# A top-2 gate that writes each row twice: rows dealt to partitions in eight contiguous blocks, stores of 8 MB, and a max/min tournament for the top two

## The chip, the cores and the metric

The kernel runs on one core of a Trainium2 chip. The metric is the device time of one execution in microseconds; before the change the median of three runs is 247.52 us (246.92 to 250.12). The profile below is one execution, whose span from the first to the last instruction is 244.7 us.

## The reference

There are 16 x 1,024 = 16,384 rows. Each has 512 numbers in `x` and 8 router logits. The two largest softmax probabilities of a row are scaled to sum to one, and the row of `x` is written out twice, once times each of the two.

```python
def reference(x, router_logits, k):          # x (16,1024,512), logits (16,1024,8), k = 2
    logits_max = np.max(router_logits, axis=-1, keepdims=True)
    probs = np.exp(router_logits - logits_max)
    probs = probs / np.sum(probs, axis=-1, keepdims=True)
    topk_indices = np.argsort(probs, axis=-1)[..., -k:]
    topk_probs = np.take_along_axis(probs, topk_indices, axis=-1)
    topk_probs = topk_probs / np.sum(topk_probs, axis=-1, keepdims=True)
    x_expanded = x[:, :, np.newaxis, :].repeat(k, axis=2)
    return (x_expanded * topk_probs[..., np.newaxis]).astype(np.float32)
```

So 33.6 MB of `x` and 0.5 MB of logits are read, and 67.1 MB are written. With two chosen, the weights are sigmoids of plus and minus the difference of the two largest logits; the smaller one comes first.

## The kernel before

Rows are dealt to the 128 partitions in one piece: partition p holds the 128 rows from 128p on. In HBM one partition's rows of `x` are 256 KB, of the output 512 KB, and that is the step from one partition to the next in each load and store.

The logits come with one load on the SP queue (line 49), 4 KB per partition. VectorE (DVE in the profile) then finds the two largest of each row in four operations over 1,024 elements per partition: the maximum (line 54), a mask of where it is (58), the logits with the maximum pushed down (62), and the maximum again (54). A subtraction gives `dlt` (71), and ScalarE (ACT) makes the two weights `WA` by sigmoids (74 and 77).

The main loop has 16 steps. Each loads 8 rows per partition of `x` into a tile `xg`, 2 MB in 128 pieces of 16 KB, on the SP queue (line 101); 16 multiplies on VectorE, one for each row and slot, write `og` (line 106); and one store from the ACT queue (line 111) sends `og`, 4 MB in 128 pieces of 32 KB. There are four buffers for `xg` and three for `og`, kept by tile pools.

The order is set by these buffers. SP issues the load of step c + 4 when the multiplies of step c are done; VectorE begins step c + 3 when the store of step c has landed; ACT issues a store when its multiplies are done. Each engine works through its own list in order, so an instruction that waits holds up all that stand behind it. Loads and stores are on two DMA queues, in the profile q1 (SP) and q10 (ACT), which share the same 16 DMA engines; 8 of a transfer's 128 partition rows fall to each of them.

Of the kernel before, what the change touches and what calls it, by code (L numbers as in the profile page):

```python
# [1 line left out]

# [4 lines left out]


@with_exitstack  # L10
def kernel(
    ctx: ExitStack,
    tc: tile.TileContext,
    x: bass.AP,
    router_logits: bass.AP,
    k: bass.AP,
    out: bass.AP,
):
    nc = tc.nc
    P = 128  # L20

    B, S, D = x.shape
    E = router_logits.shape[-1]
    K = int(k)
    N = B * S

    assert N % P == 0
    M = N // P
    assert E <= 64
    assert 2 <= K <= E  # L30

    x_v = x.rearrange("b s d -> (b s) d").rearrange("(p m) d -> p m d", p=P)
    o_v = out.rearrange("b s k d -> (b s) (k d)").rearrange(
        "(p m) d -> p m d", p=P
    )
    rl_v = router_logits.rearrange("b s e -> (b s) e").rearrange(
        "(p m) e -> p m e", p=P
    )

    wpool = ctx.enter_context(tc.tile_pool(name="wpool", bufs=1))  # L40

    L = 8
    assert M % L == 0
    NCH = M // L
    xbufs = ctx.enter_context(tc.tile_pool(name="xbufs", bufs=4))
    obufs = ctx.enter_context(tc.tile_pool(name="obufs", bufs=3))

    logits = wpool.tile([P, M, E], mybir.dt.float32)
    nc.sync.dma_start(logits, rl_v)

    V = wpool.tile([P, M, K], mybir.dt.float32)
    cur = logits
    for i in range(K):
        nc.vector.reduce_max(V[:, :, i : i + 1], cur, axis=mybir.AxisListType.X)  # L54
        if i < K - 1:
            eq = wpool.tile([P, M, E], mybir.dt.float32, tag=f"eq{i}")
            nxt = wpool.tile([P, M, E], mybir.dt.float32, tag=f"nxt{i}")
            nc.vector.tensor_tensor(  # L58
                eq, cur, V[:, :, i : i + 1].to_broadcast([P, M, E]),
                op=mybir.AluOpType.is_ge,  # L60
            )
            nc.vector.scalar_tensor_tensor(  # L62
                nxt, eq, -1.0e30, cur,
                op0=mybir.AluOpType.mult, op1=mybir.AluOpType.add,
            )
            cur = nxt

    WA = wpool.tile([P, K, M], mybir.dt.float32)
    if K == 2:
        dlt = wpool.tile([P, M], mybir.dt.float32)  # L70
        nc.vector.tensor_tensor(  # L71
            dlt, V[:, :, 0], V[:, :, 1], op=mybir.AluOpType.subtract
        )
        nc.scalar.activation(  # L74
            WA[:, 1, :], dlt, mybir.ActivationFunctionType.Sigmoid, scale=1.0
        )
        nc.scalar.activation(  # L77
            WA[:, 0, :], dlt, mybir.ActivationFunctionType.Sigmoid, scale=-1.0
        )
    else:  # L80
        Em = wpool.tile([P, M, K], mybir.dt.float32)
        nc.vector.tensor_tensor(
            Em, V, V[:, :, 0:1].to_broadcast([P, M, K]),
            op=mybir.AluOpType.subtract,
        )
        nc.scalar.activation(Em, Em, mybir.ActivationFunctionType.Exp)
        Ssum = wpool.tile([P, M], mybir.dt.float32)
        nc.vector.reduce_sum(Ssum, Em, axis=mybir.AxisListType.X)
        Rinv = wpool.tile([P, M], mybir.dt.float32)
        nc.vector.reciprocal(Rinv, Ssum)  # L90
        for slot in range(K):
            nc.vector.tensor_tensor(
                WA[:, slot, :],
                Em[:, :, K - 1 - slot],
                Rinv,
                op=mybir.AluOpType.mult,
            )

    for c in range(NCH):
        xg = xbufs.tile([P, L, D], mybir.dt.float32, tag="xg")  # L100
        nc.sync.dma_start(xg, x_v[:, c * L : (c + 1) * L, :])
        og = obufs.tile([P, L, K * D], mybir.dt.float32, tag="og")
        for l in range(L):
            m = c * L + l
            for slot in range(K):
                nc.vector.tensor_scalar_mul(  # L106
                    og[:, l, slot * D : (slot + 1) * D],
                    xg[:, l, :],
                    WA[:, slot, m : m + 1],
                )  # L110
        nc.scalar.dma_start(o_v[:, c * L : (c + 1) * L, :], og)  # L111


# [1 line left out]
_INS = ['x', 'router_logits', 'k']  # L115
_OUTS = [((16, 1024, 2, 512), 'float32')]
#: Inputs that are plain numbers.
_NUMBERS = {'k': 2}


# [26 lines left out]
```

## Time and profile before

| what | time or amount |
|---|---|
| median of three runs | 247.52 us |
| span of the profiled execution | 244.7 us |
| VectorE busy | 107.8 us, 44% of the span |
| of it the 256 multiplies of line 106 | 102.6 us, 480 ns each |
| ScalarE busy | 1.8 us |
| moved by DMA | 101.2 MB, 414 GB/s over the span |
| logits, from issue to landing | 3.4 us |
| x tile of 2 MB, from issue to landing, median | 47.0 us |
| store of 4 MB, from issue to landing, median | 36.5 us |
| first multiply starts | 9.85 us |
| first store issued | 16.31 us |

The page has the busy time of each engine, then the span in 40 equal slices, in which each digit is the busy share in tenths, then the DMA queues with their packets, bytes and the share that their packets took of the time of 16 DMA engines. A packet is the piece that a DMA engine moves at once; one semaphore write of 4 bytes per engine and transfer is counted as a packet too. A table by stretches gives for each stretch its length, the busy time of three engines with the number of instructions, the clock of TensorE (not used here), the share of time in which DMA engines were busy, and the rate in GB/s. The waits say which instruction waited for what, for how long in total, how often, and how long at most.

### The profile page before, as it was taken

The numbers are of one execution on the slowest core, as the hardware profiler recorded it, in microseconds if no ns is written. First come the engines' busy times: TensorE is split into PE (matmuls) and PEld (weight loads), VectorE is DVE, ScalarE is ACT, GpSimd is POOL, SyncE is SP. The second block draws the span as 40 slices with busy tenths as digits, with TensorE's granted clock in tenths as the row PEclk, the third lists the DMA queues.
The fourth block names the chain that finished last, engine by engine and source line by source line (L and its number), as shares of the span: only waits on it lengthen the run. The fifth ranks groups of instructions, "written<-read, shape, count | busy, mean of one in ns | idle before, by whom it ended". The sixth has DMA issues, their size and how long they took to land.

```text
span 244.7 us, 383 instructions
## 1 busy us (share of the span) xinstructions
DVE 107.8 (44%) x261; ACT 1.8 (1%) x3; POOL 0.2 (0%) x4
## 2 busy tenths in 40 slices
DVE  3999708155190641807237081551906409081000
ACT  2000000000000000000000000000000000000000
POOL 0000000000000000000000000000000000000000
DMA  7999999999999999999999999999999999999980
GB/s 279 431 431 351 469 402 435 426 429 447 426 415 439 434 434 439 412 415 463 399 423 426 429 462 421 426 437 426 466 421 394 437 453 429 429 429 429 429 375 32
DMA packets 4754, 101.21 MB, mean 414 GB/s; under 512 B 528, under 2 KB 528, under 8 KB 656
## 3 DMA queue, kind: packets, MB, share of 16 engines
q10 hardware_dynamic: 2304, 67.11, 63.8%
q1 hardware_dynamic: 2448, 34.08, 33.3%
q14 instruction: 2, 0.02, 0.0%
HBM read 34.08 MB, written 67.11 MB: 414 GB/s over the span
## 4 chain that ended last, share of the span: by engine, by line
DMA 74%; DVE 15%; issue 0%; DVEq 0%; ACT 0%; ACTq 0%
DMA out_dram<-og 54%; DMA xg<-in_x_dram 19%; DVE og L106 13%; DMA logits<-in_router_logits_dram 1%; DVE V L54 1%; DVE nxt L62 1%; DVE eq L58 1%; DVEq L142 0%; ACT WA L74 0%; DVE dlt L71 0%; DVEq L106 0%; ACTq L111 0%
## 5 line engine op out<-in xcount | busy, mean ns | idle before, releaser
L106 DVE TENSOR_SCALAR og<-xg,WA 128x512 f32<-128x512 f32 x256 | 102.6, 480 | 109.3 <-DMA out_dram<-og 108.9
L54 DVE TENSOR_REDUCE V<-logits 128x128 f32<-128x1024 f32 x1 | 1.2, 1219 | 4.2 <-DMA logits<-in_router_logits_dram 4.2
L74 ACT ACT_TABLE_LOAD x1 | 1.3, 1283 | 0.7 <-PEq L128 0.7
L62 DVE SCALAR_TENSOR_TENSOR nxt<-eq,logits 128x1024 f32<-128x1024 f32 x1 | 1.2, 1226 | 0.0
L58 DVE TENSOR_TENSOR eq<-logits,V 128x1024 f32<-128x1024 f32 x1 | 1.2, 1225 | 0.0
L54 DVE TENSOR_REDUCE V<-nxt 128x128 f32<-128x1024 f32 x1 | 1.2, 1220 | 0.0
L74 ACT ACTIVATE WA<-dlt 128x128 f32<-128x128 f32 x1 | 0.3, 309 | 7.5 <-DVE dlt L71 7.5
L71 DVE TENSOR_TENSOR dlt<-V 128x128 f32<-128x128 f32 x1 | 0.3, 292 | 0.0
L77 ACT ACTIVATE WA<-dlt 128x128 f32<-128x128 f32 x1 | 0.3, 292 | 0.0
L128 POOL MEMSET const-bfloat16-1.0<- 128x1 bf16 x1 | 0.1, 102 | 0.0
L128 POOL MEMSET const-uint8-127<- 128x1 uint8 x1 | 0.1, 102 | 0.0
L128 POOL MEMSET const-float32-0.0<- 128x1 f32 x1 | 0.1, 99 | 0.2 <-issue 0.2
L128 POOL MEMSET const-float32-1.0<- 128x1 f32 x1 | 0.1, 99 | 0.0
## 6 DMA issues: line engine op xcount, KB each, us to landing
out_dram<-og ACTq DMA_DIRECT2D x16, 4096.0 KB, 36.5
xg<-in_x_dram SPq DMA_DIRECT2D x16, 2048.0 KB, 47.0
logits<-in_router_logits_dram SPq DMA_DIRECT2D x1, 512.0 KB, 3.4
```

The lines of the kernel that those rows point to most:

```text
L54: nc.vector.reduce_max(V[:, :, i : i + 1], cur, axis=mybir.AxisListType.X)
L58: nc.vector.tensor_tensor(eq, cur, V[:, :, i : i + 1].to_broadcast([P, M, E]), op=mybir.AluOpType.is_ge,)
L62: nc.vector.scalar_tensor_tensor(nxt, eq, -1.0e30, cur, op0=mybir.AluOpType.mult, op1=mybir.AluOpType.add,)
L71: nc.vector.tensor_tensor(dlt, V[:, :, 0], V[:, :, 1], op=mybir.AluOpType.subtract)
L74: nc.scalar.activation(WA[:, 1, :], dlt, mybir.ActivationFunctionType.Sigmoid, scale=1.0)
L77: nc.scalar.activation(WA[:, 0, :], dlt, mybir.ActivationFunctionType.Sigmoid, scale=-1.0)
L106: nc.vector.tensor_scalar_mul(og[:, l, slot * D : (slot + 1) * D], xg[:, l, :], WA[:, slot, m : m + 1],)
L128: nc = _bacc.Bacc("TRN2", target_bir_lowering=False, num_devices=1)
```

## The change

The rows are dealt anew. The output is cut into eight blocks of 2,048 rows, and within a block partition p holds 16 rows in succession. One store is then one block: 8 MB that lie in HBM without a break, in 128 pieces of 64 KB. It takes 16 rows of `og` per partition, so `og` is twice as large and has two buffers instead of three; two `xg` tiles of 8 rows (as large as before, four buffers as before) fill one `og`. In HBM, the step from one partition to the next becomes 32 KB for `x` and 64 KB for the output. The logits must be dealt in the same way, and their load has 8 pieces of 512 B per partition instead of one of 4 KB.

The two largest logits are found by a tournament: halves of the eight are compared by maximum and minimum, then halves of these, so that after three rounds the first and the second stand alone. That is 2 + 4 + 4 operations on 512, 256 and 128 elements per partition. The sigmoids are as before, in the other order. The branch for more than two choices, which did not run here, is gone.

The change is meant to let stores write the output in large contiguous stretches, with fewer and larger pieces, and to find the top two with less work.

```diff
+def top2_weights(nc, pool, logits, M, E):
+    hi, lo, n = None, None, E
+    while n > 1:
+        n //= 2
+        if hi is None:
+            a, b = logits[:, :, 0:n], logits[:, :, n : 2 * n]
...
+            nc.vector.tensor_tensor(nhi, a, b, op=ALU.max)
+            nc.vector.tensor_tensor(nlo, a, b, op=ALU.min)
+        else:
+            a, b = hi[:, :, 0:n], hi[:, :, n : 2 * n]
...
+            nc.vector.tensor_tensor(tmp, lo[:, :, 0:n], lo[:, :, n : 2 * n], op=ALU.max)
+            nc.vector.tensor_tensor(nlo, a, b, op=ALU.min)
+            nc.vector.tensor_tensor(nlo, nlo, tmp, op=ALU.max)
+            nc.vector.tensor_tensor(nhi, a, b, op=ALU.max)
+        hi, lo = nhi, nlo
...
+    LS = 16
+    LX = 8
+    A = M // LS
+    x_v = x.rearrange("b s d -> (b s) d").rearrange("(a p m) d -> a p m d", a=A, p=P)
     o_v = out.rearrange("b s k d -> (b s) (k d)").rearrange(
-        "(p m) d -> p m d", p=P
+        "(a p m) d -> a p m d", a=A, p=P
     )
     rl_v = router_logits.rearrange("b s e -> (b s) e").rearrange(
-        "(p m) e -> p m e", p=P
+        "(a p m) e -> p a m e", a=A, p=P
     )
...
-    obufs = ctx.enter_context(tc.tile_pool(name="obufs", bufs=3))
+    obufs = ctx.enter_context(tc.tile_pool(name="obufs", bufs=2))
...
-    nc.sync.dma_start(logits, rl_v)
+    nc.sync.dma_start(logits.rearrange("p (a m) e -> p a m e", a=A), rl_v)
+    WA = top2_weights(nc, wpool, logits, M, E)
...
-    for c in range(NCH):
-        xg = xbufs.tile([P, L, D], mybir.dt.float32, tag="xg")
-        nc.sync.dma_start(xg, x_v[:, c * L : (c + 1) * L, :])
-        og = obufs.tile([P, L, K * D], mybir.dt.float32, tag="og")
-        for l in range(L):
-            m = c * L + l
-            for slot in range(K):
-                nc.vector.tensor_scalar_mul(
-                    og[:, l, slot * D : (slot + 1) * D],
-                    xg[:, l, :],
-                    WA[:, slot, m : m + 1],
-                )
-        nc.scalar.dma_start(o_v[:, c * L : (c + 1) * L, :], og)
+    for a in range(A):
+        og = obufs.tile([P, LS, 2 * D], F32, tag="og")
+        for h in range(LS // LX):
+            xg = xbufs.tile([P, LX, D], F32, tag="xg")
+            nc.sync.dma_start(xg, x_v[a, :, h * LX : (h + 1) * LX, :])
+            for l in range(LX):
+                r = h * LX + l
+                m = a * LS + r
+                for slot in range(2):
+                    nc.vector.tensor_scalar_mul(
+                        og[:, r, slot * D : (slot + 1) * D],
+                        xg[:, l, :],
+                        WA[:, slot, m : m + 1],
+                    )
+        nc.scalar.dma_start(o_v[a], og)
```

More of the change, by code (lines that the diff above doesn't have):

```diff
@@ L7 @@
 from concourse._compat import with_exitstack
+F32 = mybir.dt.float32
+ALU = mybir.AluOpType
+ACTF = mybir.ActivationFunctionType
+P = 128
+def top2_weights(nc, pool, logits, M, E):
[4 more added lines that the diff above has]
+            a, b = logits[:, :, 0:n], logits[:, :, n : 2 * n]
+            nhi = pool.tile([P, M, n], F32, tag=f"hi{n}")
+            nlo = pool.tile([P, M, n], F32, tag=f"lo{n}")
+            nc.vector.tensor_tensor(nhi, a, b, op=ALU.max)
+            nc.vector.tensor_tensor(nlo, a, b, op=ALU.min)
+        else:
+            a, b = hi[:, :, 0:n], hi[:, :, n : 2 * n]
+            nhi = pool.tile([P, M, n], F32, tag=f"hi{n}")
+            nlo = pool.tile([P, M, n], F32, tag=f"lo{n}")
+            tmp = pool.tile([P, M, n], F32, tag=f"tmp{n}")
+            nc.vector.tensor_tensor(tmp, lo[:, :, 0:n], lo[:, :, n : 2 * n], op=ALU.max)
[3 more added lines that the diff above has]
+        hi, lo = nhi, nlo
+    dlt = pool.tile([P, M], F32, tag="dlt")
+    nc.vector.tensor_tensor(dlt, hi[:, :, 0], lo[:, :, 0], op=ALU.subtract)
+    WA = pool.tile([P, 2, M], F32, tag="WA")
+    nc.scalar.activation(WA[:, 0, :], dlt, ACTF.Sigmoid, scale=-1.0)
+    nc.scalar.activation(WA[:, 1, :], dlt, ACTF.Sigmoid, scale=1.0)
+    return WA
 @with_exitstack
@@ L19 @@
     nc = tc.nc
-    P = 128
     B, S, D = x.shape
     E = router_logits.shape[-1]
-    K = int(k)
     N = B * S
-    assert N % P == 0
+    assert int(k) == 2 and E == 8 and N % P == 0
     M = N // P
-    assert E <= 64
-    assert 2 <= K <= E
-    x_v = x.rearrange("b s d -> (b s) d").rearrange("(p m) d -> p m d", p=P)
+    LS = 16
+    LX = 8
+    A = M // LS
+    x_v = x.rearrange("b s d -> (b s) d").rearrange("(a p m) d -> a p m d", a=A, p=P)
     o_v = out.rearrange("b s k d -> (b s) (k d)").rearrange(
-        "(p m) d -> p m d", p=P
+        "(a p m) d -> a p m d", a=A, p=P
@@ L35 @@
     )
     rl_v = router_logits.rearrange("b s e -> (b s) e").rearrange(
-        "(p m) e -> p m e", p=P
+        "(a p m) e -> p a m e", a=A, p=P
     )
     wpool = ctx.enter_context(tc.tile_pool(name="wpool", bufs=1))
-    L = 8
-    assert M % L == 0
-    NCH = M // L
     xbufs = ctx.enter_context(tc.tile_pool(name="xbufs", bufs=4))
-    obufs = ctx.enter_context(tc.tile_pool(name="obufs", bufs=3))
-    logits = wpool.tile([P, M, E], mybir.dt.float32)
-    nc.sync.dma_start(logits, rl_v)
@@ L51 @@
[L51 to L60, printed above, removed]
-            )
[L62 to L90, printed above, removed]
-        for slot in range(K):
[L92 to L97, printed above, removed]
@@ L99 @@
-    for c in range(NCH):
-        xg = xbufs.tile([P, L, D], mybir.dt.float32, tag="xg")
-        nc.sync.dma_start(xg, x_v[:, c * L : (c + 1) * L, :])
-        og = obufs.tile([P, L, K * D], mybir.dt.float32, tag="og")
-        for l in range(L):
-            m = c * L + l
-            for slot in range(K):
-                nc.vector.tensor_scalar_mul(
-                    og[:, l, slot * D : (slot + 1) * D],
-                    xg[:, l, :],
-                    WA[:, slot, m : m + 1],
-                )
-        nc.scalar.dma_start(o_v[:, c * L : (c + 1) * L, :], og)
+    obufs = ctx.enter_context(tc.tile_pool(name="obufs", bufs=2))
@@ new lines @@
+    logits = wpool.tile([P, M, E], F32)
+    nc.sync.dma_start(logits.rearrange("p (a m) e -> p a m e", a=A), rl_v)
[15 more added lines that the diff above has]
+        nc.scalar.dma_start(o_v[a], og)
```

## The prediction

> **What bounds the kernel now.** I read the page from its slices (part 2) to the queues (part 3), then the stage table, the waits, and last the chain.
>
> ```profile
> DVE  3999708155190641807237081551906409081000
> ...
> DMA  7999999999999999999999999999999999999980
> GB/s 279 431 431 351 469 402 435 426 429 447 426 415 439 434 434 439 412 415 463 399 423 426 429 462 421 426 437 426 466 421 394 437 453 429 429 429 429 429 375 32
> ...
> q10 hardware_dynamic: 2304, 67.11, 63.8%
> q1 hardware_dynamic: 2448, 34.08, 33.3%
> ```
>
> Each slice is 6.1 us. The DMA row is full from the second to the 38th slice; VectorE (DVE) is idle more than half the time. The two queues, stores (q10) and loads (q1), took 97.1% of sixteen engines' span. 67.11 MB in 32 KB rows is 2,048 packets (the other 256 are semaphore writes), so a store packet took 0.638 x 16 x 244.7 / 2,048 = 1.22 us; the 2,048 load packets of 16 KB took about 0.61. Twice the bytes, twice the time: a packet's fixed part is small. The packet records, mostly 611 and 1,213 ns, put it at 611 - (1,213 - 611) = 9 ns.
>
> ```profile
> 4.00:16.00 12.00, 11.33 (x21) 0.51 (x2) 0.00 (x0) 1.00 1.01 431
> 16.00:23.00 7.00, 7.00 (x19) 0.00 (x0) 0.00 (x0) 1.00 1.02 363
> 60.00:120.00 60.00, 25.69 (x64) 0.00 (x0) 0.00 (x0) 1.00 1.00 427
> 220.00:236.00 16.00, 1.35 (x4) 0.00 (x0) 0.00 (x0) 1.00 0.99 426
> 236.00:244.70 8.70, 0.00 (x0) 0.00 (x0) 0.00 (x0) 1.00 0.25 105
> ```
>
> These are stretches of the span; the last two columns are DMA share and GB/s. Loads alone (first row), both (third) and stores alone (fourth) all run at about 430 GB/s: one ceiling, whatever the direction. Two places are below it. At 16 to 23 us, where the first store enters (issued 16.31), 363 GB/s. At the end, engines average 0.25 x 8.7 = 2.2 us of work after 236, but the last packet ends at 243.5: a few late engines make the tail.
>
> ```profile
> DVE og L106 <- DMA out_dram<-og: 108.9, 13, 9.2
> ```
>
> The multiplies wait 109 us for buffers of finished stores, which costs nothing as long as the DMA engines have packets. Last, how the queues share an engine, in the window 60 to 120 us:
>
> ```profile
> q10 hardware_dynamic: 589, 17.20, 66.9%
> q1 hardware_dynamic: 588, 8.39, 32.9%
> ```
>
> Equal packet counts, not equal bytes; in the records of one engine load and store packets alternate. Equal counts are also forced here by the buffers, so I lean on the alternation.
>
> **What the Trainium skill says.** "DMA: Bandwidth & Descriptors", section "Where 436 GB/s comes from", puts the ceiling of the sixteen engines at 435 GB/s; the stages above, 426 to 431, agree, so there is no bandwidth left to win. The same page, "Queues, rings and completion order", says that an engine takes its queues in turn, a packet at a time; 589 against 588 agrees. Its section "Latency and other measured facts" has a loss for row pitches of megabytes in HBM, but full rate (207 GB/s each way) at 512 KiB. Stores here step 512 KB between partitions, loads 256 KB, at 427 GB/s together: no penalty for contiguity to remove. "VectorE: DVE Perf Modes", section on the TRN2 errata, gives an fp32 two-tensor operation (N+151)/0.96 ns; for N = 1,024 that is 1,224, and the trace has 1,225.
>
> **The change, part by part.**
>
> *Top two.* Four operations of 1.22 us go (4.89 us). Ten come: two of N = 512 (691 ns), four of 256 (424), four of 128 (292 by the row of dlt), together 4.25 us. Saved: 0.64 us less some 0.2 for six more starts. Beside it the engines load x, so it is worth nothing by itself.
>
> *Logits load.* 128 rows of 4 KB become 1,024 pieces of 512 B. An engine handles 56 more packets; at 9 ns that is +0.5 us of engine time in front of everything. Low end 0; high end 1.5, since the first packets of a run are slow (now 3.4 us from issue to landing). I take 0.5.
>
> *Stores.* 16 of 4 MB become 8 of 8 MB, in 64 KB rows; the program states a row as one element, so I expect one packet of 2 x 1,213 - 9 = 2,417 ns. Half as many packets, 64 fewer per engine: -0.6 us. If rows are cut in two, 0.
>
> *Buffers and turns.* This is the real change. Now a 32 KB packet alternates with a 16 KB one, just the kernel's ratio of stored to loaded bytes, and both queues stay full. Afterwards 64 KB alternates with 16 KB: a pair takes 2.42 + 0.61 = 3.03 us, a store is 8 rows per engine, 24.2 us, and exactly one x tile (8 rows) rides along. A block needs two. So the store queue must run dry at times and tiles then load alone, at 0.61 x 8 = 4.9 us each. The first multiply of a block waits, with two buffers instead of three, for the store two blocks back; behind it queue DVE's later multiplies, and for these wait the store on ACT and the reload of x on SP. None of it costs while some queue has packets. Walk: tiles 0 to 3 load by 23.4; sixteen multiplies take 6.43, so store 0 is issued at about 22.5. In the profile before, the first store was issued at 16.31 and its first packet is recorded at 20.9, about five load packets later; so packets from 27. Until then tile 4 has six of its rows. Store 0 runs to 51, store 1 to 75, with tiles 4 and 5 and most of 6; block 2 is multiplied meanwhile, and store 2 runs to 100 with tile 7 nearly done. Then loads alone, tiles 8 and 9; store 3 from about 112, 4 behind it, 5 just in time at 160; gap again near 185 to 198 for tiles 13 to 15; stores 6 and 7 back to back to the end. The engines never idle: 0 us.
>
> *Restarts.* Each time stores enter beside loads, what happened at 16 to 23 us may recur: (427 - 363) / 427 x 7 = 1.05 us. The walk has three restarts more. Low end 0 (it was a first-touch effect), high end 3.2. I take 1.6, the middle, for want of a second case in the trace.
>
> *End.* The last store's packets are followed by the same receipt; late engines keep their tail.
>
> Sum: 247.5 + 0.5 - 0.6 + 1.6 = 249.0.
>
> **Rivals.**
>
> *The tail gap (slower).* If the last x tile lands with no store left, the engines idle through its landing (about 1.2 us, as from the last packet to the span's end), sixteen multiplies (6.4) and the start of the last store (1.0, as from issue to first packet of the logits): 8.6 us, giving 257.6. For it: pairs of stores are set by a few packets, and had store 5 come a little late, store 7 would stand alone. Partial gaps give 250 to 257. Against: the walk above.
>
> *Rows of 64 KB run slower.* No such packet is in the trace. If the rate fell 4%, 101.2 MB would take 9.4 us more: 258. Against: 4, 16 and 32 KB rows show only the fixed part.
>
> *Contiguity helps.* If the slow packets at the start and the late engines vanish, 1 us and 4 to 5 us of tail go: 242. Against: late engines lag through the whole run, in the same layout as the punctual ones.
>
> *Rows cut in 32 KB.* Then alternation stays 2:1, no gaps: 247.5 + 0.5 = 248.
>
> **How the numbers follow.** No idling, with 64 KB packets or halves: 0.63 (249; halves inside it). Tail gap: 0.22, of which 0.04 stays within 2%. Slow rows: 0.09. Contiguity helps: 0.06. Two per cent is 5 us, 242.5 to 252.5. Faster 0.06; slower 0.18 + 0.09 = 0.27; same 0.67. The range 245.0 to 257.6 holds the first case with its bounds (246.9 to 251.6 and run spread), nearly all gaps and half of the slow rows, about 0.85.
>
> **What would show it.** Right: the q10 row with half the data packets at 2.4 us; slices of loads alone between stores; full DMA digits to the end; the last tile landing before about 210. Wrong: a zero DMA slice before the last store (tail gap); below 420 GB/s in stretches with stores alone (slow rows); dips after each restart of over 1 us. Most likely to upset the forecast is the pairing of stores near the end, which a few packets decide.

## The result and the profile after

The changed kernel takes 258.72 us (median of four runs, 258.3 to 263.68) against 247.22 us before: ratio 1.047, 95% interval 1.042 to 1.052. It is slower by 11.5 us. Ratios, here and below, leave out runs that were over 1.5% slower than the fastest of the same kernel (here the one of 263.68). The forecast was 249.0, with a range of 245.0 to 257.6 and no change as the likeliest outcome, so the time lies outside the range and the change is a clear slowdown. The case that came true is the first rival, the tail gap, which had been given 0.22 and 257.6 us.

The slices and the queues of the page after; a slice is now 6.4 us:

```profile
DVE  2899950063720072299700450369008460036000
...
DMA  7999999999999999999999899989999999703977
GB/s 273 427 432 412 424 444 470 419 432 388 404 429 411 449 414 381 429 432 429 429 409 406 345 397 457 383 345 460 409 391 427 450 439 452 335 38 163 490 327 327
...
q10 hardware_dynamic: 1152, 67.11, 62.1%
q1 hardware_dynamic: 3344, 34.08, 32.4%
```

Two things differ from before. Near the end the DMA row falls from 9 through 7 to 0 and 3, with 38 GB/s in one slice, where before nothing fell until the very end. The zero is the sign that the prediction named for the tail gap. And in the middle the rate falls to 345, 381 and 383 in some slices although the digits stay at 8 and 9. A slice holds few packets of 64 KB, so single slices jump; but the table by stretches below has 404 GB/s from 130 to 160 us with full engines. The engines have packets, but slower ones. The store queue now has 1,024 data packets, so a row of 64 KB is one packet: 0.621 x 16 x 256.6 / 1,024 = 2.49 us each.

Both parts can be put in numbers from the queue rows. Packets took 94.5% of 256.6 us, 242.5 us per engine, after 97.1% of 244.7, 237.6 us, before: 4.9 us more work. The rest of the span, without packets, went from 7.1 to 14.1 us: 7.0 us more idling. The sum is the 11.9 us between the two spans. (Idling is time of one engine without a packet, averaged over the sixteen.)

The waits of VectorE, longest in total first:

```profile
DVE og L90 <- DMA xg<-in_x_dram: 84.9, 8, 19.5
DVE og L90 <- DMA out_dram<-og: 39.0, 3, 18.4
```

Before, the multiplies waited for finished stores alone. Now they mostly wait for x: loads are starved, that is, they get too few turns. The table by stretches (DMA share and GB/s last), of both queues beside each other, of the end of the seventh store (store 6, counted from 0), of the gap, and of the last store alone:

```profile
130.00:160.00 30.00, 6.43 (x16) 0.00 (x0) 0.00 (x0) 1.00 1.02 404
222.00:229.00 7.00, 0.46 (x2) 0.00 (x0) 0.00 (x0) 1.00 0.26 110
229.00:235.70 6.70, 5.97 (x16) 0.00 (x0) 0.00 (x0) 1.00 0.00 0
235.70:255.40 19.70, 0.00 (x0) 0.00 (x0) 0.00 (x0) 1.00 0.99 426
```

From 229 to 235.7 no engine has a packet while VectorE multiplies the last x tile; from 222 to 229 most engines have already done their part of store 6 and wait for the late ones. That is 6.7 + 0.74 x 7.0 = 11.9 us of idling per engine. Only 7.0 of it are lost against the kernel before, because that one had idle engines at its end instead: 0.75 x 8.7 = 6.5 us after 236, where its late engines finished. Here all engines start the last store together and end it within 0.2 us. The timeline of VectorE shows what these multiplies waited for:

```profile
164.28 6.43 DVE L90 TENSOR_SCALAR og<-xg,WA 128x512 f32<-128x512 f32 x16 [12.96 <-DMA xg<-in_x_dram]
...
228.54 6.43 DVE L90 TENSOR_SCALAR og<-xg,WA 128x512 f32<-128x512 f32 x16 [18.80 <-DMA xg<-in_x_dram]
```

The semaphore records have one increment per engine and transfer, so they tell when each tile was complete on its first and on its last engine (us from the start):

```
              issued   first engine   last engine
tile 9          72.2          111.5         117.3
tile 10         98.1          116.4         139.9
tile 11        113.8          144.5         164.3
tile 15        170.7          203.2         228.5
store 6        199.8          222.5         228.7
store 7        235.0          255.6         255.8
```

Some engine had its eight rows of tile 15 at 203, just as store 6 came in (its first packet is at 202.8). The last one had to take them between the packets of store 6 and ended with it, 25 us later. A tile counts when the last engine has it.

### The profile page after: what moved, and what is told of

It is laid out like the page before. It is cut to its first block, busy times and chain, and to the rows that moved or that the text cites. A ratio compares the mean times of both kernels' runs of the same rounds, so it can differ in the third digit from the quotient of the medians.

```text
span 256.6 us, 367 instructions
## 1 busy us (share of the span) xinstructions
DVE 106.1 (41%) x267; ACT 1.8 (1%) x3; POOL 0.2 (0%) x4
## 4 chain that ended last, share of the span: by engine, by line
DMA 38%; DVE 27%; another core or an unknown queue 25%; DVEq 0%; issue 0%; SPq 0%
DVE og L90 27%; DMA xg<-in_x_dram 20%; DMA out_dram<-og 18%; SPq L78 0%; DVEq L126 0%; DVEq L90 0%
## 5 line engine op out<-in xcount | busy, mean ns | idle before, releaser
L90 DVE TENSOR_SCALAR og<-xg,WA 128x512 f32<-128x512 f32 x256 | 102.3, 481 | 123.9 <-DMA xg<-in_x_dram 84.9
L26 DVE TENSOR_TENSOR nhi<-logits 128x512 f32<-128x512 f32 x1 | 0.7, 693 | 5.0 <-DMA logits<-in_router_logits_dram 5.0
L36 DVE TENSOR_TENSOR nhi<-nhi 128x256 f32<-128x256 f32 (+1 forms) x2 | 0.7, 355 | 0.0
L34 DVE TENSOR_TENSOR nlo<-nhi 128x256 f32<-128x256 f32 (+1 forms) x2 | 0.7, 354 | 0.0
L35 DVE TENSOR_TENSOR nlo<-nlo,tmp 128x256 f32<-128x256 f32 (+1 forms) x2 | 0.7, 354 | 0.0
L33 DVE TENSOR_TENSOR tmp<-nlo 128x256 f32<-128x256 f32 (+1 forms) x2 | 0.7, 353 | 0.0
L27 DVE TENSOR_TENSOR nlo<-logits 128x512 f32<-128x512 f32 x1 | 0.7, 684 | 0.0
```

The costliest lines, as they stand in the source:

```text
L26: nc.vector.tensor_tensor(nhi, a, b, op=ALU.max)
L27: nc.vector.tensor_tensor(nlo, a, b, op=ALU.min)
L33: nc.vector.tensor_tensor(tmp, lo[:, :, 0:n], lo[:, :, n : 2 * n], op=ALU.max)
L34: nc.vector.tensor_tensor(nlo, a, b, op=ALU.min)
L35: nc.vector.tensor_tensor(nlo, nlo, tmp, op=ALU.max)
L36: nc.vector.tensor_tensor(nhi, a, b, op=ALU.max)
```

## The experiments

Theory T: packet sizes set the turns; with 64 KB against 16 KB a load row gets through only once per stored row, tiles come late, the last with the last store but one, and the engines run dry. Rivals: L, the contiguous deal slows the packets; P, 64 KB packets are slow by themselves. Ratios are to the kernel before on the same chip.

**Stores in half rows.**

```diff
-        nc.scalar.dma_start(o_v[a], og)
+        for g in range(2):
+            nc.scalar.dma_start(o_v[a][:, g * LX : (g + 1) * LX, :], og[:, g * LX : (g + 1) * LX, :])
```

> The changed kernel, but each block's store is issued as two stores of 4 MB one behind the other, once all 32 multiplies of the block are done, so that a piece is 32 KB instead of 64 KB. Deal of the rows, buffers, and the moment of every issue stay. Theory T (turns: 64 KB against 16 KB lets only one row of x pass per row stored, so x tiles come late and the last one rides with the last store but one): with 32 KB against 16 KB no starving, no zero slice before the last store, 247 to 250 us, ratio to the kernel before 1.00 to 1.01. Theory L (the contiguous deal itself slows the packets): the gap may go, but the stores stay slower, 251 to 254 us. If neither is the cause, it stays at 258.

Measured 247.4 us, ratio 1.006 (0.999 to 1.014). The loss is gone, with deal, tournament and logits as changed. But the expectation was wrong on two things. Its waits:

```profile
DVE og L90 <- DMA out_dram<-og: 72.8, 6, 12.8
DVE og L90 <- DMA xg<-in_x_dram: 37.3, 8, 5.7
```

Some waiting for x is left, 37.3 us, which costs nothing as the engines have packets meanwhile. And the trace has the first store issued after 16 multiplies (at 16.4 us), not after 32. The run changes the piece and the moment of issue together, so it needed the next one.

**One store per block, in pieces of 32 KB.** A hole of 64 B between the two halves of a partition's rows keeps them from joining.

```diff
-        og = obufs.tile([P, LS, 2 * D], F32, tag="og")
+        og = obufs.tile([P, 2, LX * 2 * D + 16], F32, tag="og")
...
-                        og[:, r, slot * D : (slot + 1) * D],
+                        og[:, h, (2 * l + slot) * D : (2 * l + slot + 1) * D],
...
-        nc.scalar.dma_start(o_v[a], og)
+        nc.scalar.dma_start(
+            o_v[a].rearrange("p (g l) d -> p g (l d)", g=2), og[:, :, 0 : LX * 2 * D]
+        )
```

> The changed kernel with one store of 8 MB per block, issued after all 32 multiplies as there, but in pieces of 32 KB: the two halves of a block's rows lie 64 B apart in the og buffer, so that they do not join. Only the size of a store's pieces differs (in the run with half rows, the first half of a block turned out to be issued already after its 16 multiplies, so that run changed the moment of issue too). Theory T (piece sizes set the turns): 246 to 250 us, no gap before the last store. If it was the later issue of whole blocks: 255 us or more.

Measured 250.39 us, ratio 1.014 (1.005 to 1.023): 0.4 us above what T allowed. Its waits, then its queues and its stretches around the end of store 6:

```profile
DVE og L90 <- DMA out_dram<-og: 109.8, 6, 21.2
...
DVE og L90 <- DMA xg<-in_x_dram: 1.2, 1, 1.2
```

```profile
q10 hardware_dynamic: 2176, 67.11, 63.8%
q1 hardware_dynamic: 3344, 34.08, 32.5%
...
215.00:225.00 10.00, 6.59 (x17) 0.00 (x0) 0.00 (x0) 1.00 0.83 357
225.00:242.00 17.00, 0.00 (x0) 0.00 (x0) 0.00 (x0) 1.00 1.00 432
242.00:249.50 7.50, 0.00 (x0) 0.00 (x0) 0.00 (x0) 1.00 0.13 57
```

The wait for x falls from 84.9 to 1.2 us with nothing changed but the piece. That is the starving, shown. Of the ratio's 0.047, the piece accounts for 0.033, some 8 us (the two ratios are from different chips). A smaller rest stays. A store of a whole block is issued late, so at 215 to 225 the early engines have nothing (share 0.83), and late engines make a tail after 242. But more than half of the rest is slow packets: of the 4.8 us between its span and that of the kernel before, 2.1 are idling and 2.7 are work (96.3% of 249.5 us after 97.1% of 244.7), although no packet here is of 64 KB. Its store packets took 3.9 us per engine more than at 1,213 ns each, in the kernel before 0.7. With halves issued as they are ready (the run above) the idling is covered and the slow packets are fewer, 1.9 us.

**The old deal with 64 KB pieces.** `x_v`, `o_v` and the logits as before the change, all else changed.

```diff
-    x_v = x.rearrange("b s d -> (b s) d").rearrange("(a p m) d -> a p m d", a=A, p=P)
+    x_v = x.rearrange("b s d -> (b s) d").rearrange("(p a m) d -> a p m d", a=A, p=P)
...
-        "(a p m) d -> a p m d", a=A, p=P
+        "(p a m) d -> a p m d", a=A, p=P
...
```

> The changed kernel with the old deal of rows (each partition 128 rows in one piece, so partitions are 512 KB apart in the output and 256 KB in x, logits loaded in 4 KB pieces), and everything else as changed: stores of 8 MB in 64 KB pieces, two og buffers, tournament. Theory T: the starving and the tail gap do not depend on where the rows lie in HBM: 255 to 259 us, with a zero slice before the last store. Theory L: 247 to 251 us.

Measured 263.83 us, ratio 1.072 (1.063 to 1.082), above what T expected. Two slices before the last store have 55 and 12 GB/s, and the multiplies wait for x:

```profile
DVE og L90 <- DMA xg<-in_x_dram: 74.7, 6, 21.6
```

The gap does not come from where rows lie: L falls as the cause of it. In its trace store 5 came later still: it was issued at 176.5, 6.3 us after store 4 had landed, where the changed kernel issued it 2.2 us before that. The 5 us beyond the changed kernel are no mark of the old deal: the changed kernel itself, measured again on another chip (last experiment), took 257 to 265 us and in its profile issued store 5 at 177.3.

**The new deal alone.** The kernel before, with 16 contiguous blocks of 8 rows per partition.

```diff
-    x_v = x.rearrange("b s d -> (b s) d").rearrange("(p m) d -> p m d", p=P)
+    x_v = x.rearrange("b s d -> (b s) d").rearrange("(a p m) d -> a p m d", p=P, m=8)
...
-        "(p m) d -> p m d", p=P
+        "(a p m) d -> a p m d", p=P, m=8
...
```

> The kernel before with the new deal of rows alone: sixteen blocks, in each of which partition p holds 8 rows in succession, so that every store is one contiguous stretch of 4 MB and every x tile one of 2 MB; logits in 512 B pieces; 32 KB and 16 KB pieces, three og buffers and the old top two as before. If contiguity is worth something: 242 us. Theory T (turns) says that only the packet sizes mattered: 246 to 249 us, ratio 1.00.

Median 253.66 us over 248.76 to 255.17, too scattered for an interval and above what either case expected. (The logits come in pieces of 256 B here, 8 rows of 32 B, not of 512 B.) No gain from contiguity. In its trace the last store is complete on the first engine at 238.6 and on the last at 249.8, where the kernel before had 237.9 and 243.8. Whether the deal makes these late engines, or they happen in any deal, this run does not tell.

**The ratio of 4 to 1 without 64 KB packets.** The kernel before, with x in pieces of 8 KB.

```diff
-        xg = xbufs.tile([P, L, D], mybir.dt.float32, tag="xg")
-        nc.sync.dma_start(xg, x_v[:, c * L : (c + 1) * L, :])
+        xg = xbufs.tile([P, 2, 4 * D + 16], mybir.dt.float32, tag="xg")
+        nc.sync.dma_start(
+            xg[:, :, 0 : 4 * D],
+            x_v[:, c * L : (c + 1) * L, :].rearrange("p (g l) d -> p g (l d)", g=2),
+        )
...
-                    xg[:, l, :],
+                    xg[:, l // 4, (l % 4) * D : (l % 4 + 1) * D],
```

> The kernel before with x loaded in pieces of 8 KB instead of 16 KB (the two halves of a tile's rows lie 64 B apart in SBUF, so they do not join), nothing else changed. Packets then alternate 32 KB against 8 KB, 4 to 1 as in the changed kernel, but without any 64 KB packet. Theory T: loads are starved, the multiplies wait for x and not for stores, and the engines idle before the last store: 250 to 257 us. Theory P (64 KB packets are the cause): 246 to 249 us.

Measured 249.87 us, ratio 1.013 (1.006 to 1.019), just under what T expected. Its longest wait, a stretch before its last store, and its queues:

```profile
DVE og L109 <- DMA xg<-in_x_dram: 81.9, 7, 17.1
```

```profile
232.00:238.00 6.00, 3.22 (x9) 0.00 (x0) 0.00 (x0) 1.00 0.44 186
...
q10 hardware_dynamic: 2304, 67.11, 63.0%
q1 hardware_dynamic: 4496, 34.08, 34.5%
```

The starving and the idle stretch appear in the old kernel from smaller load pieces alone. P is not needed for them. But they are not what makes this run longer. The stretch idles (1 - 0.44) x 6 = 3.4 us, and the last store then ends within 0.2 us on all engines instead of 5.9, so over the whole span the idling is 6.2 us, no more than the 7.1 before. What grew is work: 97.5% of 247.2, 241.0 us, 3.4 more, nearly all of it in the load packets, which are more and in part slower.

**64 KB stores beside 32 KB loads.** The changed kernel, with x tiles of 16 rows in two buffers.

```diff
-    xbufs = ctx.enter_context(tc.tile_pool(name="xbufs", bufs=4))
+    xbufs = ctx.enter_context(tc.tile_pool(name="xbufs", bufs=2))
...
+        xg = xbufs.tile([P, LS, D], F32, tag="xg")
+        if a == 0:
+            for h in range(LS // LX):
+                nc.sync.dma_start(xg[:, h * LX : (h + 1) * LX, :], x_v[a, :, h * LX : (h + 1) * LX, :])
+        else:
+            nc.sync.dma_start(xg, x_v[a])
...
```

> The changed kernel with 64 KB pieces in the stores kept, but x loaded in tiles of 16 rows (32 KB pieces, two buffers of 64 KB in all, as before), the first tile in two halves so that the multiplies can begin as early. Packets then alternate 64 KB against 32 KB, 2 to 1 as in the kernel before. Theory T: no tail gap, about 248 plus up to 2 us of idling at the start, because the third tile can only be loaded when block 0 is multiplied: 248 to 252 us. Theory P (64 KB packets are slow by themselves): the slow store packets stay, 4 to 5 us more, 252 to 256 us, with 64 KB packets of 2.7 to 3.1 us in the trace.

Measured 284.01 us, ratio 1.155 (1.146 to 1.164). Neither theory had that. Its stretch of 180 us, and its queues from 100 to 200 us:

```profile
40.00:220.00 180.00, 63.08 (x159) 0.00 (x0) 0.00 (x0) 1.00 1.00 345
```

```profile
q10 hardware_dynamic: 384, 23.07, 68.7%
q1 hardware_dynamic: 384, 11.53, 31.5%
```

Loads are not starved and the engines never idle, but they move only 345 GB/s: the packets themselves are slow, 64 KB in 2.92 us on average (2.42 alone), 32 KB in 1.40 (1.21 alone). So P is true for something. The next two runs ask for what.

> The run with x in 32 KB pieces and stores in 64 KB pieces, which took 284 us with store packets of 2.9 us on average, in the old deal of rows (512 KB between partitions in the output, 256 KB in x). If the contiguous deal makes 64 KB packets slow beside 32 KB loads: about 250 us, packets back at 2.42 us. If it is the sizes themselves: 280 to 285 us.

In the old deal 281.54 us, ratio 1.141 (1.131 to 1.151), packets of 2.90 us. The deal is not it.

> The run with x in 32 KB pieces (284 us), with each block's store issued as two stores of 32 KB pieces, so that 32 KB alternates with 32 KB. If the 64 KB packets were what slowed that run: 248 to 253 us, with packets of 1.21 us on both queues. If it is the schedule with two x tiles of 16 rows, or the 32 KB loads: 275 us or more.

With the stores in two halves of 32 KB pieces: 242.47 us, ratio 0.983 (0.974 to 0.992), below what either case expected; store packets of 1.21 us and load packets of 1.24. The slowness went with the 64 KB packet, and the run was faster than both kernels. The first half of a block is issued earlier here too (the first at 16.3 us, where the run of 284 us issued its first store at 22.5), and no run separates this from the size of the packet. Again, for a closer interval, and in the old deal:

> The run with x in 32 KB pieces and the stores in two halves of 32 KB pieces, once more, for an interval: 242 to 244 us, ratio 0.98 to the kernel before.

> The same as the run with x in 32 KB pieces and stores in two halves, in the old deal of rows. If the contiguous deal has a part in its 242.5 us: 246 us or more. If the piece sizes and the order of the transfers do it alone: 241 to 244 us.

242.35 us, ratio 0.983 (0.978 to 0.988), and in the old deal 242.51, ratio 0.983 (0.977 to 0.990). The deal of rows makes no difference in this pair. The DMA row of the first of them and two of its stretches:

```profile
DMA  6999999999999999999999999999999999999994
```

```profile
120.00:200.00 80.00, 35.88 (x91) 0.00 (x0) 0.00 (x0) 1.00 1.00 433
...
237.00:240.30 3.30, 0.00 (x0) 0.00 (x0) 0.00 (x0) 1.00 0.07 30
```

The rate stays at 433 in a stretch of both queues, and the end is short: first and last engine complete the last store 2.0 us apart, where the kernel before had 5.9. In this run 32 KB loads take turns with 32 KB stores; why the engines stay closer together was not tested.

**The tournament alone**, in the kernel before.

> The kernel before with the tournament alone in place of the four operations that find the two largest. The prediction holds it for hidden behind the loading of x: ratio 0.995 to 1.005, the first multiply about 0.5 us earlier.

Measured 249.15 us, ratio 1.010 (1.003 to 1.017), where 0.995 to 1.005 was expected. The first multiply came 0.4 us earlier (9.45 for 9.85). The first engine completes the last store at 238.1, as before (237.9); the last at 246.9 instead of 243.8. The tournament ends before 9 us, and I know of no way from there to an engine that is late at 240. I take it for the same unexplained spread of late engines as with the new deal alone, and this is an argument, not a test. It does show that the tournament brings no gain.

**The last stores cut, the others left.** First the last block alone, its halves issued as they are multiplied:

```diff
-        nc.scalar.dma_start(o_v[a], og)
+            if a == A - 1:
+                nc.scalar.dma_start(
+                    o_v[a][:, h * LX : (h + 1) * LX, :], og[:, h * LX : (h + 1) * LX, :]
+                )
+        if a < A - 1:
+            nc.scalar.dma_start(o_v[a], og)
```

> The changed kernel, but the store of the last block alone is cut into two halves, each issued when its 16 multiplies are done; all before is the same. Theory T: the first half (4 MB, 9.8 us of the engines' time) is queued about when the sixth store still runs and fills the gap of about 7 us before the last store: 251 to 253 us, 7 less than the changed kernel. If the gap is not what costs, it stays at 257 to 259 us.

Measured 255.86 us (252.17 to 258.71), ratio 1.032 (1.018 to 1.046), above the 251 to 253 expected. By the ratios 1.047 and 1.032 some 4 us come back, in an interval that reaches from almost none to the 7 us expected. The first half did fill the gap, but the second still waited for the last tile's multiplies (issued 237.8), and engines done early with the first half had nothing again. So the last three blocks were cut, beside the changed kernel on one chip:

```diff
-        nc.scalar.dma_start(o_v[a], og)
+        if a < A - 3:
+            nc.scalar.dma_start(o_v[a], og)
+        else:
+            for g in range(2):
+                nc.scalar.dma_start(
+                    o_v[a][:, g * LX : (g + 1) * LX, :], og[:, g * LX : (g + 1) * LX, :]
+                )
```

> The changed kernel, but the stores of the last three blocks go out in two halves of 32 KB pieces each; blocks 0 to 4 keep stores of 8 MB in 64 KB pieces. If the 11.5 us by which the changed kernel is slower are about 7 us of idling before the last store and about 4.5 us of slow packets while 64 KB pieces run beside loads, this takes the first part away and leaves most of the second: 250 to 253 us, no slice near zero before the end, multiplies of blocks 2 to 5 still waiting for x. If the late tiles of the middle cost time by themselves: 254 us or more.

> The changed kernel once more on the same chip, to compare with: 257 to 260 us, engines idle before the last store.

Both scattered on that chip, and both medians lie above what was expected: 250.57 to 256.65 (median 255.54) and 257.42 to 264.72 (median 262.88), so no interval came of it. The lowest of each are 6.9 us apart, which agrees with 7 us of idling taken away. Above the lowest of the kernel before (244.39) 6.2 us are left, more than the 4.5 us of slow packets that were expected to stay. In the profile of the first no slice before the end is near zero, as expected. With one run of each to compare this supports the split, and does not prove it.

## Why the prediction was wrong

*Ceiling and what bounds the kernel: right.* Loads alone (4 to 16 us) run at 431 GB/s and the last store alone at 426 to 429, and contiguity brought nothing: 0.983 and 0.983 in the two deals.

*Top two: right that it is worth nothing, mis-sized.* Operations of 0.69, 0.42 and 0.29 us, as worked out. But each starts before the one ahead of it has ended (0.60 to 0.61, 0.33 and 0.20 us apart), so the ten took 3.48 us up to the subtraction, where the four had taken 5.03: 1.55 us saved and not some 0.4. The first multiply still starts at 9.95 us, not earlier than before (9.85), because the first x tile now lands last (9.85).

*Logits: slightly high.* +0.5 us of engine time was forecast. 64 packets of 27 ns are 1.74 us per engine, after 8 of 205 ns, 1.64, before: +0.1. Against the median of 159 ns the eight would have taken 1.27, so the forecast of +0.5 was right for the packets' fixed part; it left out that some first packets before were slow.

*Packet size and turns: right.* 64 KB in one packet of 2.418 us (forecast 2.417), taking turns with load packets. In the window 130 to 160 us:

```profile
q10 hardware_dynamic: 165, 9.76, 83.0%
q1 hardware_dynamic: 160, 2.36, 18.5%
```

*The walk: this is the step that failed.* It ended in "The engines never idle: 0 us"; measured 7.0 us more of idling. Its beginning held (store 0's first packet at 26.7, forecast 27; stores 0, 1, 2 landed at 53, 79 and 105, forecast 51, 75 and 100). What it had wrong is store 5 "just in time at 160", and with it the pairing of stores at the end.

Its own costs do not give that time. At 112 some 14 rows of tiles 10 and 11 were still to load, beside stores, at 3.03 us each: to about 154. With 1.2 us for the landing, 6.4 of multiplies and the 4.6 from issue to first packet that it had taken for store 0, store 5's packets would begin near 167 (an estimate from the walk's numbers), 7 us after the end of store 4.

The trace adds a second thing: the walk moved all sixteen engines as one. When stores come back after a stretch of loads alone, a row that an engine has still to load costs it 2.42 + 0.61 us instead of 0.61. The first engine took 4.9 us from the end of tile 9 to the end of tile 10, the last one 22.6 us, 2.8 a row. (The records do not name the engine, so that the last is the same one both times is inferred.) So the last engine completes tile 10 23.5 us after the first, tile 11 19.8, tile 15 25.3, and VectorE waits for the last. Tile 11 was there at 144.5 on the first engine and at 164.3 on the last.

Store 5 was issued at 170.7, and its first packet is at 175.0. Tile 13 then came beside store 5, at 193.3, so store 6 was issued at 199.8, before store 5 had landed. No gap was left for tile 15, which should have come "near 185 to 198"; it came with store 6 at 228.5, and store 7 stood alone. The prediction had this as a rival, with the condition for it (store 5 "a little late") and 8.6 us of idling; the time with no packet at all is from 228.5 to 235.8, the first packet of store 7: 7.3 us. How much of the delay of store 5 is the walk's arithmetic and how much the spread of the engines, no run separates. That the rival's 257.6 us lay so near the measured 258.7 is in part luck: its idling was too large and it had no slow store packets.

*The buffers.* "None of it costs while some queue has packets" held: of the waits for x, 84.9 us in all, those in the middle left the engines busy (digits of 8 and 9). It is where the weight should have been laid, since both queues ran empty at the last tile, which VectorE had only when the slowest engine had loaded it.

*Restarts: right in size, with some luck.* 1.6 us were taken, between 0 and 3.2, for "three restarts more", though the walk shows only two, at 112 and after 198. What load packets took over 0.611 us adds up to 3.1 us per engine, before 1.55: 1.5 more. Of the 3.1, 2.7 are in bunches at 24 to 32, 72 to 80, 112 to 120 and 168 to 176 us, where stores enter.

*Slow store packets: missing from the sum.* Slow rows of 64 KB were a rival, at 0.09 and 9.4 us. Store packets took 2.487 us on average instead of 2.418: 4.4 us per engine over the whole run, after 0.7 in the kernel before, so +3.7. It comes on top of the idling, so two rivals that were kept apart came together. Alone the packets are not slow: the last store, with no loads beside it, moved its 8.39 MB from 235.8 to 255.4, 429 GB/s. But beside loads of 16 KB it is not shown that the 64 KB are the reason. Packets of 32 KB lost 3.9 us with one store per block and 3.7 with the new deal alone, each in one trace; the reason stays open.

Sum: 0.1 for logits, -0.5 for the fixed part of half as many store packets, +1.5 at restarts, +3.7 for slow store packets, which is 4.8 us of work; 7.0 us of idling; together 11.8, for 11.9 between the spans.

## What to carry to other kernels

Where loads and stores share DMA engines that take turns by packet, the piece sizes set how the rate is split. Compare the ratio of the pieces with the ratio of bytes that the kernel needs, here two stored for one loaded. With store pieces four times the load pieces the multiplies waited 84.9 and 81.9 us for x, with twice 37.3 us or less, with equal pieces 8.1 and 8.7. The ratio is not all: 64 KB beside 32 KB starved nothing and was the slowest of all.

Full engines for most of the span are no proof that nothing is lost. Look at the last load: after it only multiplies stand between an empty queue and the last store. Stores cut into parts at the end got some of that time back here. In a hand-worked schedule of transfers, carry every delay through to the end, and count a tile as complete when the slowest engine has it: ask what one late packet costs that engine in the next phase.

## What the runs showed of the hardware that was not expected

Stores in 64 KB packets beside loads in 32 KB packets slowed both: 345 GB/s for 180 us with all engines busy (store packets 2.92 us for 2.42, load packets 1.40 for 1.21), in either deal of the rows; with 32 KB stores, the first half of each block issued earlier, the kernel ran at 427 to 434 GB/s. Why is open.

Sixteen engines with the same work end at different times, and in the runs with 32 KB stores and no idle stretch before the last one, this is the whole difference between their spans. The first engine completes the last store at nearly the same time in all of them, and the span ends 0.9 us after the last engine:

| run | span, us | first engine | last engine | store packets, over 1,213 ns, us per engine |
|---|---|---|---|---|
| x in 32 KB, half stores, again | 240.3 | 237.4 | 239.4 | 0.05 |
| the same, first time | 241.0 | 238.0 | 240.1 | 0.1 |
| the same in the old deal | 240.9 | 238.1 | 240.0 | 0.5 |
| the kernel before | 244.7 | 237.9 | 243.8 | 0.7 |
| stores in half rows | 246.1 | 237.9 | 245.3 | 1.9 |
| the tournament alone | 247.7 | 238.1 | 246.9 | 1.9 |
| the new deal alone | 250.7 | 238.6 | 249.8 | 3.7 |

The last column is the time that all store packets took beyond their usual 1,213 ns, divided by sixteen. It goes with the lateness, so the late engines are probably those with the slow packets; the records do not name a packet's engine, so this is not shown. Each row is one trace. It is not the deal of rows alone: the new deal has the smallest value and the largest. What slows a packet was not found.
